# Token layout of a two-layer hybrid backbone: 1154 columns with a gap between the segments, or 1152 columns without one

## The chip, the cores and the metric

The kernel runs on one core of one Trainium2 chip. The metric is the device time of one execution in microseconds (us), as the median of several executions. A core has a matmul engine (PE, with weight loads PEld that overlap the matmuls), three engines for elementwise work (DVE, ACT, POOL), and queues for DMA (SP among them). Each engine works through its own instructions in order and waits on semaphores for the others.

## The reference

Two layers of a diffusion backbone run for two groups of tokens that share all weights: 1024 latent tokens and 128 context tokens, each of 1024 channels. Each layer adds a gated mixer and then a gated feed-forward network (FFN) with a depthwise convolution over three neighbouring tokens. Each group has its own conditioning vector, and a convolution must not reach from one group into the other.

```python
for l in range(DEPTH):                      # 2 layers
    m_ctx = modulation(c_ctx[None, :], w_mod[l], b_mod[l])
    m_lat = modulation(c, w_mod[l], b_mod[l])
    h_ctx = adaln(ctx, g_norm_mix[l], m_ctx[0], m_ctx[1])
    h_lat = adaln(lat, g_norm_mix[l], m_lat[0], m_lat[1])
    # l = 0: latent attention | gMLP;  l = 1: convolution (31 taps) | pooling
    ctx = ctx + m_ctx[2] * mix_ctx
    lat = lat + m_lat[2] * mix_lat
    ctx = ctx + m_ctx[5] * conv_ffn(adaln(ctx, ...), ...)
    lat = lat + m_lat[5] * conv_ffn(adaln(lat, ...), ...)

def conv_ffn(h, w_in, w_dw, b_dw, w_out):   # 1024 -> 2 x 2816 -> 1024
    z = depthwise_conv(h @ w_in, w_dw, b_dw)    # 3 taps, zeros outside the segment
    g, u = z[..., :D_FF], z[..., D_FF:]
    return (jax.nn.silu(g) * u) @ w_out
```

## The kernel before

Activations are held with channels on the partitions and tokens along the row. A row has T = 1154 columns: 1024 latent tokens, two columns of zeros, and 128 context tokens from column CX = 1026. The row is worked in three blocks (BLK): columns 0 to 383, 384 to 767, and 768 to 1153. The third block, block 2, is 386 wide: 256 latent tokens, the two zero columns, 128 context tokens. The normed input `hb` is one tile a block, with rows of BW = 386.

All large products take fp32 operands as a sum of two parts (`split`: ACT writes the high part, L83 or L87; DVE the low part, L84 or L88), and `mm3` (L76 to L78) makes three matmuls for each pair of tiles. Weights come by DMA (`raw`), and `unit_split` splits them too (L66 on ACT, L67 on DVE).

The stages follow one another: norm and projections of layer 0 (`even_kv`, `even_q`, `even_gate`), attention, output projection with the residual and the next norm (`out_half`, `out_blocks`, `norm_blk`), FFN of layer 0 (`ffn`), `odd` for layer 1's mixer, and the FFN of layer 1. In an FFN 44 channel tiles of 128 (22 pairs, g and u) are made one after another; the two tiles of a pair are called its halves. For a half, `products` makes 24 matmuls a block into a PSUM tile (`fps`), and ACT copies each block into the row tile `z` (L405). Two z buffers exist. `half` then scales the row on ACT (L412, the middle tap with the bias) and adds the two neighbours on DVE, over the whole row (L414, L416): the two zero columns keep the segments apart and give the zeros at their ends. `pair` applies SiLU to g (L423) and multiplies (L426), `keep` splits the product (L83, L84) into `act`, and `outp` multiplies two or three of these by the output weights (`ops`), with the residual on DVE (L383, two pieces in block 2).

The two zero columns must be zero wherever a row passes through matmuls: DVE clears them in `hb` (L315, four times), POOL in `gmo`, `att`, `pd` and the convolution's output (L851, L525, L1055, L1251). Their products are zero, so `z` has them without a further instruction.

During the first FFN, DVE also computes later modulation vectors (`mod_fill`, L157), spread between other work by `drip`. Their sums are folded through DRAM, and POOL adds the parts when the DMAs have landed (L167, L168). POOL also adds squares for the norms (L270, L272) and takes the power in the reciprocal root (L589). The order of instructions on each engine is laid out by the tile framework's scheduler, which simulates a time line (`schedule_with_timeline_sim=True`) and takes the ready instruction of the earliest program order; `drip` puts its work later by an offset. A write to a buffer waits for the readers of the tile that had it before.

Of the kernel before, what the change touches and what calls it, by code (L numbers as in the profile page):

```python
# [19 lines left out]
P = 128  # L20
D = 1024
KT = 8
LAT = 1024
CTX = 128
CX = 1026
T = 1154
BLK = [(0, 384), (384, 384), (768, 386)]
BW = 386
TOK = [(i * 128) for i in range(8)] + [CX]
DFF = 2816  # L30
NPAIR = DFF // P
# [12 lines left out]
class Net:  # L44
# [250 lines left out]
    def norm_blk(self, x, l, w, b, hb, pool, big=None, inplace=False):  # L295


        nc = self.nc
        c0, n = BLK[b]
        big = big or {"nsum": (pool, "nsum"), "nsq": (pool, "nsq"), "nt": (pool, "nt")}  # L300

        def tmp(kind):
            p, tag = big[kind]
            return p.tile([P, BW], F32, tag=tag, name=self.nm(kind))

        add, rstd = self.sq_sums([0, 128, 256] if b < 2 else [0, 128, CX - 768], tmp, fast=inplace and b in FASTB)

        rbs = []

        def chain():  # L310
            rbs.append(rstd(D, pool))

        segs = [(0, 384, 0, 0)] if b < 2 else [(0, 256, 0, 0), (CX - 768, 128, 256, 1)]
        if b == 2:
            nc.vector.memset(hb[:, :, :, 256:258].bitcast(F32), 0.0)  # L315

        def scale(out, k, o, m, ro, c):
            nc.vector.scalar_tensor_tensor(out=out, in0=x[:, k, c0 + o:c0 + o + m], scalar=self.scl[l][w][:, k, c:c + 1],
                                           in1=rbs[0][:, ro:ro + m], op0=ALU.mult, op1=ALU.mult)

        def shift(src, k, o, m, c):
            so = 0 if w == 0 else 24
            self.split(hb[:, 0, k, o:o + m], hb[:, 1, k, o:o + m], src, self.mod[l][:, so + k, c:c + 1])

        def rest():
            for k in range(KT):
                for (o, m, ro, c) in segs:
                    t = tmp("nt")[:, :m]
                    scale(t, k, o, m, ro, c)
                    shift(t, k, o, m, c)  # L330

        def scaled():
            for k in range(KT):
                for (o, m, ro, c) in segs:
                    scale(x[:, k, c0 + o:c0 + o + m], k, o, m, ro, c)

        def shifted():
            for k in range(KT):
                for (o, m, ro, c) in segs:
# [47 lines left out]
    def ffn(self, x, l, hb, first, norm=None, after=None, ahead=None):  # L387
        nc, tc, ap = self.nc, self.tc, self.ap
        with ExitStack() as es:
# [4 lines left out]

            def products(tis):

                wz = [(first.pop(0) if first else self.unit(ap["fin"][l, ti]), zp.tile([P, T], F32, tag="z", name=self.nm("z")))
                      for ti in tis]
                for b, (c0, n) in enumerate(BLK):
                    for (wt, z) in wz:  # L400
                        ps = self.gp.tile([P, 512], F32, tag="gp", name=self.nm("fps"))
                        for k in range(KT):
                            self.mm3(ps[:, :n], wt[:, 0, k * P:(k + 1) * P], wt[:, 1, k * P:(k + 1) * P],
                                     hb[b][:, 0, k, :n], hb[b][:, 1, k, :n], k == 0, k == KT - 1)
                        nc.scalar.activation(z[:, c0:c0 + n], ps[:, :n], AF.Copy)  # L405
                return [z for (_, z) in wz]

            def half(ti, i, z=None):
                z = z or products([ti])[0]
                c = cp.tile([P, T], F32, tag="c", name=self.nm("c"))  # L410
                w = self.fdw
                nc.scalar.activation(c, z, AF.Identity, bias=w[:, l, ti, 3:4], scale=w[:, l, ti, 1:2])  # L412
                self.drip(1 if i > 1 else 2)
                nc.vector.scalar_tensor_tensor(out=c[:, 1:T], in0=z[:, 0:T - 1], scalar=w[:, l, ti, 0:1], in1=c[:, 1:T],  # L414
                                               op0=ALU.mult, op1=ALU.add)
                nc.vector.scalar_tensor_tensor(out=c[:, 0:T - 1], in0=z[:, 1:T], scalar=w[:, l, ti, 2:3], in1=c[:, 0:T - 1],  # L416
                                               op0=ALU.mult, op1=ALU.add)
                return c

            def pair(i):  # L420
                zs = products([i, NPAIR + i]) if i < 2 else [None, None]
                g = half(i, i, zs[0])
                nc.scalar.activation(g, g, AF.Silu)  # L423
                self.drip(4 if i > 1 else 8)
                u = half(NPAIR + i, i, zs[1])
                nc.vector.tensor_tensor(out=u, in0=g, in1=u, op=ALU.mult)  # L426
                return u

            def keep(i, u):
                a = cp.tile([P, 2, T], F32R, tag="act", name=self.nm("act"))  # L430
# [32 lines left out]
    def even(self):  # L463
# [5 lines left out]
        with ExitStack() as e1:  # L469
# [45 lines left out]
            with tc.tile_pool(name="at0", bufs=1, side="right", reuse_waits="tile") as p0:  # L515
# [6 lines left out]
                self.drip(1000)  # L522
                self.mod_scale(0, 1)
                att = left.enter_context(tc.tile_pool(name="att", bufs=1, reuse_waits="tile")).tile([P, 4, T], F32, name="att")
                nc.gpsimd.memset(att[:, :, LAT:CX], 0.0)  # L525
                qk = self.att_split(self.hpool, "h2", raw, nc.vector)
                nc.vector.tensor_copy(att[:, :, CX:T], attc)
        self.close("w")
# [317 lines left out]
    def even_gate(self, hb, gmo, w1, w2):  # L846
# [1 line left out]
        nc, ap = self.nc, self.ap  # L848
        load = lambda n, s: self.load(n, s, w1)
        ggv, bs, wst = load("ggv", [P, 512]), load("bs", [P, 512]), load("wst", [P, 4, P])  # L850
        nc.gpsimd.memset(gmo[:, :, LAT:CX], 0.0)  # L851
        wC = [self.unit(ap["evC"][:, s * 1024:(s + 1) * 1024]) for s in range(4)]

        def spatial(gi, vg):
# [186 lines left out]
    def odd(self, x, l, hb, ready):  # L1041
        nc, tc, ap = self.nc, self.tc, self.ap
        with ExitStack() as es:
# [6 lines left out]
            with ExitStack() as e0:  # L1050
# [4 lines left out]
                nc.gpsimd.memset(pd[:, :, LAT:CX], 0.0)  # L1055
                with ExitStack() as e1:
                    w1 = e1.enter_context(tc.tile_pool(name="ow1", bufs=1, reuse_waits="tile"))

# [23 lines left out]
                    def conv_in(i, then=None):  # L1082
# [14 lines left out]

                        def glu(b, ps):
                            c0 = BLK[b][0]
                            for (s, d, n) in ([(0, PADL + c0, 384)] if b < 2 else [(0, PADL + 768, 256), (258, 2 * PADL + LAT, 128)]):  # L1100
                                nc.vector.tensor_tensor(out=cv[:, d:d + n], in0=ps[:, s:s + n], in1=sg[:, c0 + s:c0 + s + n], op=ALU.mult)

                        if i == 0:
# [14 lines left out]
                    def pool(g):  # L1118
                        xp = w1.tile([P, 1184], F32, tag="sg", name=self.nm("xp"))

                        def evac(b, ps):
                            c0 = BLK[b][0]
                            for (s, d, n) in ([(0, 8 + c0, 384)] if b < 2 else [(0, 8 + 768, 256), (258, 24 + LAT, 128)]):
                                nc.scalar.activation(xp[:, d:d + n], ps[:, s:s + n], AF.Copy)

                        proj(evac)
# [119 lines left out]
    def conv_tail(self, b, co, dw, cat, tp, np_, early):  # L1246
        nc = self.nc
        c0 = BLK[b][0]
        segs = [(c0, 0, 384)] if b < 2 else [(768, 0, 256), (COX, CX - 768, 128)]
        if b == 2:  # L1250
            nc.gpsimd.memset(cat[:, :, :, 256:258].bitcast(F32), 0.0)  # L1251
        add, rstd = self.sq_sums([0, 128, 256], lambda kind: (tp if kind == "nsq" else np_).tile([P, BW], F32, tag=kind, name=self.nm(kind)),
                                 have=None if b else early)
        for i in range(0 if b else 3, 4):
# [216 lines left out]
```

## Time and profile before

| | |
|---|---|
| median of 3 runs | 2791.72 us (2788.92 to 2794.14) |
| the profiled execution | 2793.62 us, its span 2791.4 us |
| granted TensorE clock, mean | 0.983 |
| PE busy | 2704.9 us, 15636 matmuls |
| DVE busy | 1839.2 us, 2864 instructions |
| ACT busy | 998.7 us, 1671 instructions |
| POOL busy | 394.6 us, 497 instructions |

The span runs from the first to the last instruction; the execution's own time is 2.2 us longer. A row of the grouped view reads: line, engine, operation, tile written and tiles read, shape, count, then busy time in us, mean duration in ns, and the idle time of the engine just before, with what ended it. A row of a timeline reads: start and duration in us, engine, line, operation, tiles, shape, count, and in brackets the idle time before it. Consecutive rows of one kind are merged.

### The profile page before, as it was taken

The page shows a single profiled execution, that of the slowest core. Times are in us where ns is not written, and L with a number is a line of the kernel's source. Part 1 is how long each engine was busy: PE and PEld are TensorE (multiplying, and loading weights), DVE is VectorE, ACT ScalarE, POOL GpSimd, SP SyncE. Part 2 cuts the span into 40 slices and gives each one's busy share as a digit, 9 for nine tenths or more (in the row PEclk, how much of TensorE's full clock was granted, in tenths as well). Part 3 has the DMA queues.
Part 4 walks back from the last instruction along what each step waited for, and adds up shares of the span by engine and source line. Part 5 has one row for each costly group of instructions (what it writes and reads, how often), then busy time and mean ns, then how long its engine had stood idle before and what let it go on. Part 6 is the DMA issues. An engine that isn't in the chain of part 4 may idle for free.

```text
span 2791.4 us, 38552 instructions
## 1 busy us (share of the span) xinstructions
PE 2704.9 (97%) x15636; PEld 2632.4 (94%) x15636; DVE 1839.2 (66%) x2864; ACT 998.7 (36%) x1671; POOL 394.6 (14%) x497
## 2 busy tenths in 40 slices
PE   7999999999999999999999999989999999999999
PEld 3897989999999999999999999889999999999999
DVE  5873777787786778855553878987555455554445
ACT  3543278782443222222223331324422222222331
POOL 2354165640200000000000200002000000000000
PEclk9999989999999999999999999999999999999999
DMA  7254210006143444311111011010011111111111
GB/s 277 71 151 110 86 37 24 25 11 226 55 125 117 132 129 130 120 46 46 38 46 38 10 46 39 27 53 28 26 40 44 41 43 41 44 38 39 46 46 68
DMA packets 92848, 192.63 MB, mean 69 GB/s; under 512 B 9472, under 2 KB 43136, under 8 KB 92672
## 3 DMA queue, kind: packets, MB, share of 16 engines
q1 hardware_dynamic: 92672, 190.18, 21.6%
q8 instruction: 123, 2.02, 0.3%
q14 instruction: 53, 0.43, 0.1%
HBM read 170.20 MB, written 19.95 MB: 68 GB/s over the span
## 4 chain that ended last, share of the span: by engine, by line
PE 85%; DVE 8%; ACT 2%; DMA 2%; POOL 1%; issue 1%; SPq 0%; DVEq 0%; ACTq 0%; POOLq 0%
PE fps L76 13%; PE fps L77 13%; PE fps L78 13%; PE ops L76 9%; PE ops L77 9%; PE ops L78 9%; PE av L989 2%; PE ptp L978 2%; PE ips L76 1%; PE ips L77 1%; PE ips L78 1%; PE Sa L1002 1%; DVE macc L157 1%; PE Sa L1004 1%; PE Sa L1003 1%
## 5 line engine op out<-in xcount | busy, mean ns | idle before, releaser
L77 PE MATMUL fps<-h,wt 128*128 128x384 f32 (+1 forms) x2112 | 713.2, 338 | 0.0
L76 PE MATMUL fps<-h,wt 128*128 128x384 f32 (+1 forms) x2112 | 711.2, 339 | 1.8 <-ACT h L87 0.9
L78 PE MATMUL fps<-h,wt 128*128 128x384 f32 (+1 forms) x2112 | 712.5, 338 | 0.0
L383 DVE SCALAR_TENSOR_TENSOR x<-ops,mod,x 128x384 f32<-128x384 f32 (+1 forms) x832 | 395.4, 512 | 233.7 <-PE ops L78 231.7
L67 DVE TENSOR_TENSOR wt<-raw,wt 128x1024 fp32r<-128x1024 f32 (+2 forms) x177 | 216.4, 1233 | 391.8 <-ACT wt L66 391.1
L77 PEld LDWEIGHTS fps<-h,wt 128*128 128x128 f32 x2112 | 398.6, 189 | 0.3
L76 PEld LDWEIGHTS fps<-h,wt 128*128 128x128 f32 x2112 | 396.2, 188 | 2.7 <-ACT h L87 1.2
L78 PEld LDWEIGHTS fps<-h,wt 128*128 128x128 f32 x2112 | 398.1, 189 | 0.1
L78 PE MATMUL ops<-act,wt 128*128 128x384 f32 (+1 forms) x1056 | 358.2, 339 | 0.0
L77 PE MATMUL ops<-act,wt 128*128 128x384 f32 (+1 forms) x1056 | 357.0, 338 | 0.0
L76 PE MATMUL ops<-act,wt 128*128 128x384 f32 (+1 forms) x1056 | 355.4, 339 | 0.0
L405 ACT ACTIVATE z<-fps 128x384 f32<-128x384 f32 (+1 forms) x264 | 128.9, 492 | 604.6 <-PE fps L78 604.2
L66 ACT ACTIVATE wt<-raw 128x1024 fp32r<-128x1024 f32 (+2 forms) x177 | 182.9, 1047 | 439.3 <-PE ops L78 322.6
L157 DVE SCALAR_TENSOR_TENSOR macc<-mraw,sc,macc 128x512 f32<-128x512 f32 x280 | 210.8, 783 | 41.5 <-DMA mraw<-in_wmod_dram 40.8
L76 PEld LDWEIGHTS ops<-act,wt 128*128 128x128 f32 x1056 | 199.6, 189 | 0.0
L78 PEld LDWEIGHTS ops<-act,wt 128*128 128x128 f32 x1056 | 198.6, 188 | 0.1
L77 PEld LDWEIGHTS ops<-act,wt 128*128 128x128 f32 x1056 | 198.7, 188 | 0.0
L1200 DVE SCALAR_TENSOR_TENSOR co<-cv,c_odw,co 128x1168 f32<-128x1168 f32 x92 | 132.8, 1446 | 21.0 <-ACT co L1193 20.2
L76 PE MATMUL ops<-h,wt 128*128 128x384 f32 (+1 forms) x384 | 133.1, 353 | 11.5 <-ACT wt L66 7.2
L414 DVE SCALAR_TENSOR_TENSOR c<-z,fdw,c 128x1153 f32<-128x1153 f32 x88 | 127.7, 1452 | 8.6 <-ACT c L412 7.7
L83 ACT ACTIVATE act<-c 128x1154 fp32r<-128x1154 f32 x44 | 51.5, 1172 | 226.7 <-DVE c L426 182.3
L77 PE MATMUL ops<-h,wt 128*128 128x384 f32 (+1 forms) x384 | 132.2, 344 | 0.4 <-DVE h L84 0.4
(281 smaller groups left out, 4550.7 us busy)
## 6 DMA issues: line engine op xcount, KB each, us to landing
raw<-in_fin_dram SPq DMA_DIRECT2D x88, 512.0 KB, 3.5
mraw<-in_wmod_dram SPq DMA_DIRECT2D x160, 256.0 KB, 2.8
raw<-in_fout_dram SPq DMA_DIRECT2D x44, 512.0 KB, 3.5
mraw<-in_wmod_dram SPq DMA_DIRECT2D x16, 512.0 KB, 9.0
fold<-macc SPq DMA_DIRECT2D x14, 512.0 KB, 3.0
macc<-fold SPq DMA_DIRECT2D x56, 128.0 KB, 3.1
x<-in_xt_dram SPq DMA_DIRECT2D x4, 1536.0 KB, 8.9
raw<-in_odin_dram SPq DMA_DIRECT2D x12, 512.0 KB, 3.5
```

The source lines that it names most:

```text
L66: nc.scalar.activation(wt[:, 0, :n], raw[:, :n], AF.Copy)
L67: nc.vector.tensor_tensor(out=wt[:, 1, :n], in0=raw[:, :n], in1=wt[:, 0, :n].bitcast(F32), op=ALU.subtract)
L76: mm(out, wh, ah, start=start, stop=False)
L77: mm(out, wh, al, start=False, stop=False)
L78: mm(out, wl, ah, start=False, stop=stop)
L157: nc.vector.scalar_tensor_tensor(out=a[:, c, :], in0=raw, scalar=self.sc[:, k, c:c + 1], in1=a[:, c, :], op0=ALU.mult, op1=ALU.add)
L383: nc.vector.scalar_tensor_tensor(out=xs, in0=ps[:, o:o + w], scalar=self.mod[l][:, gch * 8 + m, c:c + 1], in1=xs, op0=ALU.mult, op1=ALU.add)
L405: nc.scalar.activation(z[:, c0:c0 + n], ps[:, :n], AF.Copy)
L414: nc.vector.scalar_tensor_tensor(out=c[:, 1:T], in0=z[:, 0:T - 1], scalar=w[:, l, ti, 0:1], in1=c[:, 1:T], op0=ALU.mult, op1=ALU.add)
L978: nc.tensor.transpose(tp[:, a * P:(a + 1) * P], probs[j][:, kt * P:(kt + 1) * P], self.ident)
L989: nc.tensor.matmul(av[:, :256].rearrange("p (j t) -> p j t", j=2), V[:, kt, h, :], rhs, start=(kt == 0 and part == 0), stop=(kt == 8 and p ...
L1200: nc.vector.scalar_tensor_tensor(out=o, in0=cv[:, j:j + COW], scalar=dw[:, j:j + 1], in1=o, op0=ALU.mult, op1=ALU.add)
```

## The change

The row becomes T = 1152 columns, with the context tokens from column 1024, and all three blocks are 384 wide. Only the FFN's z and c tiles keep the gap: they have ZT = 1154 columns and the context part at ZX = 1026. POOL clears the two columns of each z (88 times), the evacuation of block 2 is made in two pieces (256 and 128 columns), and the product of g and u is made in two pieces that close the gap again. The fills of `hb`, `gmo`, `att`, `pd` and the convolution's output go.

```diff
-CX = 1026
-T = 1154
-BLK = [(0, 384), (384, 384), (768, 386)]
-BW = 386
+CX = 1024
+T = 1152
+BLK = [(0, 384), (384, 384), (768, 384)]
+BW = 384
+ZX = CX + 2
+ZT = T + 2
...
-        if b == 2:
-            nc.vector.memset(hb[:, :, :, 256:258].bitcast(F32), 0.0)
...
-                wz = [(first.pop(0) if first else self.unit(ap["fin"][l, ti]), zp.tile([P, T], F32, tag="z", name=self.nm("z")))
+                wz = [(first.pop(0) if first else self.unit(ap["fin"][l, ti]), zp.tile([P, ZT], F32, tag="z", name=self.nm("z")))
                       for ti in tis]
+                for (_, z) in wz:
+                    nc.gpsimd.memset(z[:, LAT:ZX], 0.0)
...
-                        nc.scalar.activation(z[:, c0:c0 + n], ps[:, :n], AF.Copy)
+                        for (o, d, m) in [(0, c0, n)] if b < 2 else [(0, c0, 256), (256, ZX, CTX)]:
+                            nc.scalar.activation(z[:, d:d + m], ps[:, o:o + m], AF.Copy)
...
-                c = cp.tile([P, T], F32, tag="c", name=self.nm("c"))
+                c = cp.tile([P, ZT], F32, tag="c", name=self.nm("c"))
...
-                nc.vector.scalar_tensor_tensor(out=c[:, 1:T], in0=z[:, 0:T - 1], scalar=w[:, l, ti, 0:1], in1=c[:, 1:T],
+                nc.vector.scalar_tensor_tensor(out=c[:, 1:ZT], in0=z[:, 0:ZT - 1], scalar=w[:, l, ti, 0:1], in1=c[:, 1:ZT],
...
-                nc.vector.tensor_tensor(out=u, in0=g, in1=u, op=ALU.mult)
-                return u
+
+                for (d, o, m) in ((0, 0, LAT), (CX, ZX, CTX)):
+                    nc.vector.tensor_tensor(out=u[:, d:d + m], in0=g[:, o:o + m], in1=u[:, o:o + m], op=ALU.mult)
+                return u[:, :T]
...
-                nc.gpsimd.memset(att[:, :, LAT:CX], 0.0)
...
-        nc.gpsimd.memset(gmo[:, :, LAT:CX], 0.0)
...
-                nc.gpsimd.memset(pd[:, :, LAT:CX], 0.0)
...
-        if b == 2:
-            nc.gpsimd.memset(cat[:, :, :, 256:258].bitcast(F32), 0.0)
```

In `odd`, the offsets of the context part within block 2 go from 258 to 256.

More of the change, by code (lines that the diff above doesn't have):

```diff
@@ L413, in half @@
                 self.drip(1 if i > 1 else 2)
-                nc.vector.scalar_tensor_tensor(out=c[:, 1:T], in0=z[:, 0:T - 1], scalar=w[:, l, ti, 0:1], in1=c[:, 1:T],
+                nc.vector.scalar_tensor_tensor(out=c[:, 1:ZT], in0=z[:, 0:ZT - 1], scalar=w[:, l, ti, 0:1], in1=c[:, 1:ZT],
                                                op0=ALU.mult, op1=ALU.add)
-                nc.vector.scalar_tensor_tensor(out=c[:, 0:T - 1], in0=z[:, 1:T], scalar=w[:, l, ti, 2:3], in1=c[:, 0:T - 1],
+                nc.vector.scalar_tensor_tensor(out=c[:, 0:ZT - 1], in0=z[:, 1:ZT], scalar=w[:, l, ti, 2:3], in1=c[:, 0:ZT - 1],
                                                op0=ALU.mult, op1=ALU.add)
@@ L1099, in glu @@
                             c0 = BLK[b][0]
-                            for (s, d, n) in ([(0, PADL + c0, 384)] if b < 2 else [(0, PADL + 768, 256), (258, 2 * PADL + LAT, 128)]):
+                            for (s, d, n) in ([(0, PADL + c0, 384)] if b < 2 else [(0, PADL + 768, 256), (256, 2 * PADL + LAT, 128)]):
                                 nc.vector.tensor_tensor(out=cv[:, d:d + n], in0=ps[:, s:s + n], in1=sg[:, c0 + s:c0 + s + n], op=ALU.mult)
@@ L1122, in evac @@
                             c0 = BLK[b][0]
-                            for (s, d, n) in ([(0, 8 + c0, 384)] if b < 2 else [(0, 8 + 768, 256), (258, 24 + LAT, 128)]):
+                            for (s, d, n) in ([(0, 8 + c0, 384)] if b < 2 else [(0, 8 + 768, 256), (256, 24 + LAT, 128)]):
                                 nc.scalar.activation(xp[:, d:d + n], ps[:, s:s + n], AF.Copy)
```

## The prediction

> **What bounds the kernel now.** First the page: its span, the busy time of each engine, and the chain of work that ended last.
>
> ```profile
> span 2791.4 us, 38552 instructions
> ...
> PE 2704.9 (97%) x15636; PEld 2632.4 (94%) x15636; DVE 1839.2 (66%) x2864; ACT 998.7 (36%) x1671; POOL 394.6 (14%) x497
> ...
> PE 85%; DVE 8%; ACT 2%; DMA 2%; POOL 1%; issue 1%; SPq 0%; DVEq 0%; ACTq 0%; POOLq 0%
> ```
>
> The reader is to see that the matmul engine is busy nearly the whole span and that 85% of the last chain runs through it. Next the table of stretches, with each engine's busy time and instruction count, for the two feed-forward layers and for the norm between layer 0 and layer 1.
>
> ```profile
> core 0: us, PE busy (x) PEld busy (x) DVE busy (x) ACT busy (x) POOL busy (x), PEclk, DMA share, GB/s
> ...
> 800.00:1560.00 760.00, 760.00 (x4331) 759.85 (x4330) 498.59 (x693) 215.10 (x262) 33.79 (x22) 1.00 0.27 84
> 1560.00:1625.00 65.00, 57.63 (x307) 52.87 (x306) 58.51 (x119) 33.89 (x65) 18.02 (x23) 0.99 0.04 14
> ...
> 1960.00:2791.00 831.00, 825.49 (x4684) 824.59 (x4682) 427.76 (x576) 234.35 (x294) 0.00 (x0) 1.00 0.13 43
> ```
>
> In the FFN stretches PE never rests (760.00 of 760.00, 825.49 of 831.00) while DVE, ACT and POOL have much free time. There the time is the number of matmuls times their step, and nothing else. In the stretch 1560:1625 it is different: PE has 7.4 us without work and DVE is busy for 58.5 of 65 us.
>
> **The change, part by part.** *The matmuls of block 2 lose two columns.* The grouped view that keeps shapes apart counts them, one of three equal lines (L76, L77, L78) for each tile:
>
> ```profile
> L78 PE MATMUL fps<-h,wt 128*128 128x386 f32 x704 | 239.1, 340 | 0.0
> ...
> L78 PE MATMUL ops<-act,wt 128*128 128x386 f32 x352 | 119.8, 340 | 0.0
> ...
> L77 PE MATMUL ops<-h,wt 128*128 128x386 f32 x128 | 44.1, 345 | 0.4 <-DVE h L84 0.4
> ...
> L77 PE MATMUL ips<-h,wt 128*128 128x386 f32 x96 | 33.0, 344 | 0.5 <-DVE h L88 0.5
> ...
> L76 PE MATMUL ups<-h,wt 128*128 128x386 f32 x32 | 11.0, 345 | 0.3 <-ACT ug L898 0.3
> ...
> L77 PE MATMUL qps<-h,wt 128*128 128x386 f32 x24 | 8.2, 342 | 0.0
> ```
>
> That is 3 x (704 + 352 + 128 + 96 + 32 + 24) = 4008 matmuls. The mean of 340 ns is of no use here, since matmuls overlap; the step from one to the next is wanted. In the FFN an evacuation (L405) starts as soon as 24 matmuls of its block are done, so its starts in ACT's timeline are a clock for the step:
>
> ```profile
> 1519.78 0.49 ACT L405 ACTIVATE z<-fps 128x386 f32<-128x386 f32 x1 [3.75 <-PE fps L78]
> ...
> 1524.01 0.49 ACT L405 ACTIVATE z<-fps 128x384 f32<-128x384 f32 x1 [1.55 <-PE fps L78]
> ...
> 1528.22 0.49 ACT L405 ACTIVATE z<-fps 128x384 f32<-128x384 f32 x1 [1.59 <-PE fps L78]
> ...
> 1532.47 0.49 ACT L405 ACTIVATE z<-fps 128x386 f32<-128x386 f32 x1 [3.76 <-PE fps L78]
> ```
>
> Block 1 (384) took 4.21 us, block 2 (386) 4.25, block 0 after a block 2 took 4.23; a half of an FFN pair is 12.69 us. The second block is dearer by 0.04 us, so 0.04 / 24 = 1.7 ns a matmul, and 4008 x 1.7 = 6.7 us. This is my value. The upper end charges block 0's 0.02 us to the two columns as well: 0.06 / 24 = 2.5 ns, 10.0 us. The lower end comes from other widths, in PE's timeline:
>
> ```profile
> 231.15 0.40 PE L872 MATMUL vps<-wt,h 128*128 128x512 f32 x1
> ...
> 234.17 0.40 PE L873 MATMUL vps<-wt,h 128*128 128x512 f32 x1
> ...
> 346.10 0.29 PE L1003 MATMUL Sa<-qk 96*128 96x288 f32 x1
> ...
> 346.62 0.29 PE L1004 MATMUL Sa<-qk 96*128 96x288 f32 x1
> ```
>
> The first two rows lie 13 steps of 512 columns apart (232 ns each), the last two 4 steps of 288 (130 ns). The slope is (232 - 130) / 224 = 0.46 ns a column, 0.9 ns for two, 3.6 us in all. I stay with 1.7 ns because its rows are the very matmuls that shrink.
>
> The Trainium skill, page "TensorE: Matmul & The Clock Gate", section "Back-to-back issue gap", gives an isolated warm gap of N/2.4 + 2.5 ns. By it two columns are worth 0.83 ns and the sum would be an estimated 3.3 us, near the lower end above.
>
> *Copies and products that are split in two.* L405 of block 2 becomes 256 and 128 columns (88 times), L426 becomes 1024 and 128 (44 times). The grouped view prices them:
>
> ```profile
> L405 ACT ACTIVATE z<-fps 128x386 f32<-128x386 f32 x88 | 43.3, 495 | 296.2 <-PE fps L78 296.2
> ...
> L980 ACT ACTIVATE PT<-ptp 128x512 fp32r<-128x512 f32 x128 | 73.8, 596 | 19.4 <-PE ptp L978 17.5 <-ACT P L953 0.3
> ...
> L980 ACT ACTIVATE PT<-ptp 128x256 fp32r<-128x256 f32 x32 | 12.4, 388 | 0.0
> ...
> L426 DVE TENSOR_TENSOR c<-c,c 128x1154 f32<-128x1154 f32 x44 | 59.7, 1356 | 0.9
> ...
> L67 DVE TENSOR_TENSOR wt<-raw,wt 128x1024 fp32r<-128x1024 f32 x173 | 212.9, 1241 | 388.2 <-ACT wt L66 387.5 <-PE tp L701 0.6
> ...
> L273 DVE TENSOR_TENSOR nsum<-nsum,nsq 128x384 f32<-128x384 f32 x23 | 13.5, 588 | 22.8 <-POOL nsq L272 22.8
> ```
>
> L980 is the same kind of PSUM copy: 596 - 388 = 208 ns for 256 columns, so 128 columns take about 284. A split evacuation costs 388 + 284 - 495 = 177 ns more, 15.6 us of ACT in 88. For DVE, (1241 - 588) / 640 = 1.02 ns a column puts 128 columns near 327; 1241 + 327 - 1356 = 212 ns more, 9.3 us in 44. Both lie beside matmuls: ACT is busy 215 of 760 us, DVE 499. Without that cover the two would cost 25 us. One place has none, the start of an FFN, where the second pair of z waits for the first:
>
> ```profile
> 780.67 0.88 ACT L405 ACTIVATE z<-fps 128x386 f32<-128x386 f32 x2 [5.22 <-PE fps L78]
> ...
> 788.37 1.28 ACT L423 ACT_TABLE_LOAD   x1 [1.14 <-DVE c L416]
> ...
> 790.74 1.23 ACT L405 ACTIVATE z<-fps 128x384 f32<-128x384 f32 x3
> ...
> L76 PE MATMUL fps<-h,wt 128*128 128x384 f32 x1408 | 476.7, 339 | 0.9 <-ACT z L405 0.9
> ```
>
> Two L405 of block 2 stand ahead of L412, L416 and the next L405, for which PE sat idle 0.9 us. There 2 x 0.177 = 0.35 us come through; with as much in layer 1's FFN (bound: nothing), +0.7 us.
>
> *88 zero fills of z on POOL, and the fills that go.* A POOL fill of about this size takes 0.11 us, one of the removed DVE fills 0.09:
>
> ```profile
> 1523.95 1.42 DVE L416 SCALAR_TENSOR_TENSOR c<-z,fdw,c 128x1153 f32<-128x1153 f32 x1
> 1532.51 0.09 DVE L315 MEMSET h<- 128x32 f32 x1 [7.14 <-PE fps L78]
> 1533.52 0.62 DVE L383 SCALAR_TENSOR_TENSOR x<-ops,mod,x 128x384 f32<-128x384 f32 x1 [0.93 <-PE ops L78]
> ...
> 1618.91 0.10 POOL L1055 MEMSET pd<- 128x8 f32 x1 [14.09 <-DVE h L88]
> 1618.96 0.11 POOL L1094 MEMSET cv<- 128x15 f32 x1
> ```
>
> 88 x 0.11 = 9.7 us of POOL, which is busy 33.8 us in the first FFN and not at all in the second. The fill adds a wait. It cannot start before the last reader of that z buffer, and L412 on ACT waits for it, with L405 and the weight copies L66 queued behind. The reader L416 of the z evacuated at 1519.78 ends at 1525.4; the buffer's next z is complete two halves later, at 1519.78 + 2 x 12.69 = 1545.2. So the fill has 19.8 us. Queued behind it on POOL are the folds' adds (L167, L168), and in the norms L272 and the pow of the rstd. I take nothing. Of the removed fills, the one at 1532.51 held DVE for 7.14 us, but the next instruction waits for PE's first out tile anyway. The DMAs keep their number and queue, and those of block 2 move 0.5% less; I count nothing.
>
> **Sum.** -6.7 + 0.7 = -6.0 us. The profiled execution took 2793.6 us, 2.2 more than its span, and would come to 2787.6. It lies 1.9 above the median of the runs shown, so the median goes from 2791.7 to **2785.7 us**. With the two ends of the column price and 0 to 0.7 for the chain, the forecast's own range is 2781.7 to 2788.8. A measurement of this kernel can tell about 0.2%, 5.6 us, from no change, so the bound lies at 2786.1, almost on the forecast.
>
> **Rivals.** *The step is not set by columns.* A weight load takes longer than the step:
>
> ```profile
> L78 PEld LDWEIGHTS fps<-h,wt 128*128 128x128 f32 x2112 | 398.1, 189 | 0.1
> ```
>
> 189 ns against 4.21 / 24 = 175 ns. If loads set the pace, two columns fewer give nothing, and 0.7 us of chain is left: 2792.4. Against it, the step follows the width (130, 175, 232 ns for 288, 384, 512). The Trainium skill says, in the same section, that in a stream of weight loads and matmuls the spacing is set by both; the steps above do not show the load as the limit at 288 columns and more.
>
> *Norms start earlier.* With the fills L315, L1055 and their like gone, DVE and POOL are free sooner. The stretch 1560:1625 has 7.4 us of idle PE; half of it would make 2785.7 - 3.7 = 2782.0, all of it 2778.3. For it speaks that DVE is the bound there; against it that the instruction behind L315 waited for PE and that the fills behind L1055 were ended by the same norm.
>
> *Slower: the fill comes late.* POOL works in order, and a fold's add can hold what stands behind it:
>
> ```profile
> 696.58 0.53 ACT L257 ACTIVATE nsq<-x 128x384 f32<-128x384 f32 x1 [0.62 <-DVE x L383]
> ...
> 699.20 1.28 POOL L167 TENSOR_TENSOR macc<-macc 128x512 f32<-128x512 f32 x1 [3.80 <-DMA macc<-fold]
> ...
> 701.26 1.01 POOL L272 TENSOR_TENSOR nsq<-nsq,nsq 128x384 f32<-128x384 f32 x1
> ```
>
> The add L272 had its input at 697.1 and ran at 701.3, 4.2 us late, behind L167. A z fill held so would stop L412, behind it L405, and then PE. It decides from a hold of 19.8 us in steady work, and from zero at an FFN's start, where z is short. For slower than 2797.3 some 11.6 us must be lost; three holds of 4.2 us uncovered make 2785.7 + 12.6 = 2798.3. Against it: the cover is over four times the hold that the trace shows.
>
> **How the numbers follow.** Forecast 0.62 (of it 0.55 faster by over 0.2%, since the bound cuts it nearly in half), step not by columns 0.12, earlier norms 0.13, late fill 0.13. Faster: 0.62 x 0.55 + 0.13 = 0.47. Slower: 0.13. Within 0.2%: 0.28 + 0.12 = 0.40. The order on each engine is laid out anew by the kernel's scheduler from its own durations, which moves small waits both ways; the range, from the earlier norms to the first rival, has some 2 us on its upper side for that: 2778 to 2794.
>
> **What would show it.** Right: all fps, act and ups rows at 384 columns, evacuations of block 2 4.21 us after block 1's, a half of 12.63 us, L405 rows of 256 and 128 columns near 388 and 284 ns, 88 POOL fills of z with hardly any ACT idle put down to them. Wrong: a half still at 12.69; PE idle in 800:1560 that ends on z or on a POOL fill; the stretch 1560:1625 grown or shrunk by several us.

## The result, and the profile after

| | before | after |
|---|---|---|
| median | 2792.8 us (2788.9 to 2794.9, 6 runs) | 2774.6 us (2771.9 to 2776.2, 6 runs) |
| ratio | 1 | 0.9935, 95% interval 0.9922 to 0.9947 |
| the profiled execution | 2793.6 us | 2771.9 us |

The change saves 18 us. The forecast was 6 us, and the time lies below its range. The page of the kernel after, with the rows that answer to the first ones of before:

```profile
span 2770.1 us, 39051 instructions
...
PE 2678.3 (97%) x15636; PEld 2605.9 (94%) x15636; DVE 1842.8 (67%) x2904; ACT 1000.8 (36%) x1759; POOL 398.9 (14%) x581
...
PE 77%; DVE 6%; ACT 2%; DMA 2%; issue 1%; POOL 0%; DVEq 0%; SPq 0%; ACTq 0%; POOLq 0%
```

The span is 21.3 us shorter, and PE is busy 26.6 us less for the same 15636 matmuls; so PE rests 5.3 us longer (91.8 instead of 86.5 us). The table of stretches has this row for the first feed-forward layer (columns as before):

```profile
800.00:1560.00 760.00, 760.00 (x4398) 760.00 (x4397) 508.05 (x726) 219.02 (x308) 36.79 (x64) 1.00 0.27 84
```

In the same 760 us, PE never resting, 4398 matmuls start instead of 4331. Two columns fewer in a third of them, at 1.7 ns, would have given some 4331 x 0.57 / 175 = 14 more, not 67. The grouped view with shapes apart shows the added pieces:

```profile
L407 ACT ACTIVATE z<-fps 128x256 f32<-128x256 f32 x88 | 33.9, 385 | 281.6 <-PE fps L80 281.6
L407 ACT ACTIVATE z<-fps 128x128 f32<-128x128 f32 x88 | 24.1, 274 | 0.0
...
L430 DVE TENSOR_TENSOR c<-c,c 128x1024 f32<-128x1024 f32 x44 | 53.7, 1220 | 0.9
...
L430 DVE TENSOR_TENSOR c<-c,c 128x128 f32<-128x128 f32 x44 | 13.6, 309 | 0.0
...
L399 POOL MEMSET z<- 128x2 f32 x88 | 8.7, 100 | 1228.8 <-DVE c L418 1195.3
```

They cost what was forecast (385 and 274 ns for 388 and 284; 309 for 327; a fill 0.10 us for 0.11), and no instruction in the profile waited for a fill. The gain is in the matmuls. The timeline of PE has a row for each, and its start gives the step. Before, the first and the last of 170 matmuls of layer 1's FFN, which take in all three blocks:

```profile
2299.81 0.34 PE L77 MATMUL fps<-h,wt 128*128 128x384 f32 x1
...
2329.60 0.34 PE L78 MATMUL fps<-h,wt 128*128 128x386 f32 x1
```

After, the first and the last of 76 of the same kind, and of the 108 output matmuls behind them in the window:

```profile
2299.81 0.33 PE L80 MATMUL fps<-h,wt 128*128 128x384 f32 x1
...
2312.81 0.33 PE L80 MATMUL fps<-h,wt 128*128 128x384 f32 x1
2312.98 0.34 PE L78 MATMUL ops<-act,wt 128*128 128x384 f32 x1
...
2331.88 0.34 PE L80 MATMUL ops<-act,wt 128*128 128x384 f32 x1
```

Before: 29.79 / 169 = 176.3 ns. After: 13.00 / 75 = 173.3 ns on `hb`, and 18.90 / 107 = 176.6 ns on `act`. The single steps differ too: before, they waver between 168 and 184 ns in this window; after, those on `hb` are all 173 or 174 ns, while those on `act` go back and forth between 174 and 179 or 180. Below, a step is the mean time from one matmul's start to the next one's over all matmuls of a kind in such a timeline, without the few steps over 250 ns, which are waits. By kind of product, with every step that is a wait counted as one of 175 ns, the differences between the two traces add up as follows, to about 20.9 of the 21.3 us:

| product | matmuls | step before | step after | us |
|---|---|---|---|---|
| `fps<-h` (FFN in) | 6336 | 176.2 | 173.4 | -17.6 |
| `ops<-h` (mixers out) | 1152 | 176.6 | 173.6 | -3.3 |
| `ops<-act` (FFN out) | 3167 | 176.1 | 175.2 | -3.1 |
| `ips<-h` (odd mixer in) | 864 | 176.3 | 173.8 | -2.0 |
| all others | | | | -1.3 |
| waits of PE | | | | +6.5 |

In the FFN, block 2 went from 176.9 to 173.4 ns. But blocks 0 and 1, whose matmuls were 384 wide before and after, went from 175.8 to 173.4 ns. That is what the forecast did not have, and the experiments look for its cause. The largest of the changed waits are taken up in the section on the prediction.

### The profile page after: what moved, and what is told of

Its sections match the earlier page's. It is cut to its first block, busy times and chain, and to the rows that moved or that the text cites. A ratio compares the mean times of both kernels' runs of the same rounds, so it can differ in the third digit from the quotient of the medians.

```text
span 2770.1 us, 39051 instructions
## 1 busy us (share of the span) xinstructions
PE 2678.3 (97%) x15636; PEld 2605.9 (94%) x15636; DVE 1842.8 (67%) x2904; ACT 1000.8 (36%) x1759; POOL 398.9 (14%) x581
## 4 chain that ended last, share of the span: by engine, by line
PE 77%; DVE 6%; ACT 2%; DMA 2%; issue 1%; POOL 0%; DVEq 0%; SPq 0%; ACTq 0%; POOLq 0%
PE fps L78 13%; PE fps L79 13%; PE fps L80 13%; PE ops L78 8%; PE ops L79 8%; PE ops L80 8%; PE av L991 2%; PE ptp L980 2%; PE ips L79 1%; PE ips L78 1%; PE ips L80 1%; DMA mraw<-in_wmod_dram 1%; PE Sa L1004 1%; PE Sa L1006 1%; PE Sa L1005 1%; ACT P L955 1%
## 5 line engine op out<-in xcount | busy, mean ns | idle before, releaser
L78 PE MATMUL fps<-h,wt 128*128 128x384 f32 x2112 | 702.6, 335 | 3.3 <-ACT z L407 3.0
L80 PE MATMUL fps<-h,wt 128*128 128x384 f32 x2112 | 705.4, 334 | 0.0
L79 PE MATMUL fps<-h,wt 128*128 128x384 f32 x2112 | 705.1, 334 | 0.0
L80 PE MATMUL ops<-act,wt 128*128 128x384 f32 x1056 | 357.1, 338 | 0.0
L79 PE MATMUL ops<-act,wt 128*128 128x384 f32 x1056 | 356.9, 338 | 0.0
L78 PE MATMUL ops<-act,wt 128*128 128x384 f32 x1056 | 356.2, 339 | 0.0
L159 DVE SCALAR_TENSOR_TENSOR macc<-mraw,sc,macc 128x512 f32<-128x512 f32 x280 | 211.7, 786 | 53.6 <-DMA mraw<-in_wmod_dram 53.1
L399 POOL MEMSET z<- 128x2 f32 x88 | 8.7, 100 | 1228.8 <-DVE c L418 1195.3
L85 ACT ACTIVATE act<-c 128x1152 fp32r<-128x1152 f32 x44 | 51.5, 1171 | 240.7 <-DVE c L430 196.6
L78 PE MATMUL ops<-h,wt 128*128 128x384 f32 x384 | 131.2, 348 | 6.2 <-ACT h L85 4.3
L416 DVE SCALAR_TENSOR_TENSOR c<-z,fdw,c 128x1153 f32<-128x1153 f32 x88 | 124.6, 1417 | 8.7 <-ACT c L414 7.8
```

The costliest lines, as they stand in the source:

```text
L78: mm(out, wh, ah, start=start, stop=False)
L79: mm(out, wh, al, start=False, stop=False)
L80: mm(out, wl, ah, start=False, stop=stop)
L159: nc.vector.scalar_tensor_tensor(out=a[:, c, :], in0=raw, scalar=self.sc[:, k, c:c + 1], in1=a[:, c, :], op0=ALU.mult, op1=ALU.add)
L416: nc.vector.scalar_tensor_tensor(out=c[:, 1:ZT], in0=z[:, 0:ZT - 1], scalar=w[:, l, ti, 0:1], in1=c[:, 1:ZT], op0=ALU.mult, op1=ALU.add)
```

## The experiments

The change that the diff doesn't show as one is in `hb`. It is a tile of 2 x 8 rows a block (two parts, eight channel groups), and each row is the moving operand of a matmul. With BW = 386 rows lie 1544 bytes apart, with 384 they lie 1536 bytes apart. Addresses below are those of the compiled program, in bytes within a partition.

### Row distance alone, and width alone

**e1_pitch386**: the kernel after, with the rows of `hb` 386 columns apart again. All matmuls stay 384 wide, and the order of instructions on PE, DVE, ACT and POOL is the same.

```diff
-        return [self.hpool.tile([P, 2, KT, BW], F32R, tag=f"h{b}", name=self.nm(f"h{b}")) for b in range(3)]
+        return [self.hpool.tile([P, 2, KT, 386], F32R, tag=f"h{b}", name=self.nm(f"h{b}")) for b in range(3)]
```

> The changed kernel with one thing undone: the rows of hb are 386 columns apart again (1544 bytes), while every block keeps 384 columns. Theory COLUMNS (two columns fewer in block 2 made the gain, the addresses do not matter): no change against the changed kernel, 2774.6 us, FFN step 173.4 ns. Theory ADDRESS (rows 1536 bytes apart put every moving operand of hb at the same place within 128 bytes, and the step depends on that place): the step of fps goes back to a mean of 175.8 ns in all three blocks, 8856 matmuls x 2.4 ns = 21 us at most, so 2789 to 2796 us; what then is left below the kernel before is the price of the columns alone.

Measured: 2791.8 us (10 runs), ratio to before 0.9998, interval 0.9989 to 1.0008. The whole gain is gone. In its timeline of PE, the first and the last of 138 matmuls of layer 1's FFN:

```profile
2299.76 0.33 PE L78 MATMUL fps<-h,wt 128*128 128x384 f32 x1
...
2323.73 0.34 PE L80 MATMUL fps<-h,wt 128*128 128x384 f32 x1
```

23.97 / 137 = 175.0 ns. This profiled execution took 2785.6 us, the fastest of its ten, so the others must have had longer steps or waits. What follows: the gain comes with the distance of the rows; without it the two columns, with the copies and fills that they need, leave nothing in the medians. Two reservations. The longer `hb` also moves `act`, whose step in layer 0 went from 173.6 to 176.6 ns (1584 x 3.0 = 4.8 us of the loss). And e1 doesn't price the two columns by themselves: its one trace has 175.1 ns on `hb` in the FFN, against 175.8 and 176.9 before, but its rows also walk through other places than those of before (from 0 to 120 and 128 to 248 bytes above the weights' place modulo 256, where before had 64 to 184 and 192 to 312).

**e7_width386**: the kernel after, with the FFN's matmuls of block 2 made over 386 columns (the last two belong to the next row and aren't used; one in 24 stays at 384).

```diff
-                            self.mm3(ps[:, :n], wt[:, 0, k * P:(k + 1) * P], wt[:, 1, k * P:(k + 1) * P],
-                                     hb[b][:, 0, k, :n], hb[b][:, 1, k, :n], k == 0, k == KT - 1)
+                            w = 386 if b == 2 else n
+                            wl = w if k < KT - 1 else n
...
+                            mm(ps[:, :w], wh_, flat[:, k * BW:k * BW + w], start=k == 0, stop=False)
+                            mm(ps[:, :wl], wh_, flat[:, (KT + k) * BW:(KT + k) * BW + wl], start=False, stop=False)
+                            mm(ps[:, :w], wl_, flat[:, k * BW:k * BW + w], start=False, stop=k == KT - 1)
```

> The changed kernel with the width alone undone in the FFN: the 2112 fps matmuls of block 2 stream 386 columns again, the last two into PSUM columns that nothing reads (they are the head of the next row; one of 24 stays at 384). Pitch and places are those of the changed kernel. Width counts by itself: 2112 x 1.7 = 3.6 us more (at 0.83 to 0.9 ns: 1.9 us), 2776 to 2778 us, blocks 0 and 1 stay at 173.4 ns. Theory EQUAL STREAMS (the fast step needs equal widths as well as one pitch): blocks 0 and 1 go back to some 176 ns too, 6336 x 2.5 = 16 us more, 2790 us.

Measured: 2783.9 us, ratio 0.9965 (0.9951 to 0.9979), 9.3 us more than after. In ACT's timeline the evacuations of blocks 0, 1, 2 and 0:

```profile
1488.54 0.49 ACT L413 ACTIVATE z<-fps 128x384 f32<-128x384 f32 x1 [1.42 <-PE fps L411]
1492.70 0.49 ACT L413 ACTIVATE z<-fps 128x384 f32<-128x384 f32 x1
1496.95 0.55 ACT L413 ACTIVATE z<-fps 128x256 f32<-128x256 f32 x2 [3.77 <-PE fps L411]
1501.12 0.49 ACT L413 ACTIVATE z<-fps 128x384 f32<-128x384 f32 x1 [1.42 <-PE fps L411]
```

Block 2 takes 4.25 us, the others 4.16 and 4.17. Over the trace 386 columns step at 177.0 ns and 384 at 173.65 (173.4 in the kernel after), so two columns cost 3.4 to 3.6 ns, 2112 x 3.6 = 7.6 us, where the rows lie well. There the width counts too, at twice the forecast's price. The 9.3 us are not this price alone. With this edit the scheduler also laid out the instructions in another order. In the trace, the slowest of the five executions, the steps on `act` in layer 1 went from 176.7 to 173.4 ns, 5 us less, though nothing there had moved, and PE's waits grew by 12 us.

**e2_before_pitch384**: the kernel before, with the rows of blocks 0 and 1 1536 bytes apart, and block 2 as it was. A pad puts the rows at the weights' place modulo 128.

```diff
-        return [self.hpool.tile([P, 2, KT, BW], F32R, tag=f"h{b}", name=self.nm(f"h{b}")) for b in range(3)]
+        return [self.hpool.tile([P, 2, KT, (384, 384, 386)[b]], F32R, tag=f"h{b}", name=self.nm(f"h{b}")) for b in range(3)]
...
+            self.hpool.tile([P, 16], F32, name="pad")
```

> The kernel before with one thing of the change: the rows of hb of blocks 0 and 1 are 384 columns apart, with a pad of 64 bytes ahead so that they start at 96 modulo 128 as in the changed kernel; block 2 keeps its 386 columns and its row pitch. COLUMNS: no change, 2792.8 us. ADDRESS: blocks 0 and 1 step at 173.4 ns, block 2 stays near 177; 5904 matmuls x 2.4 ns = 14 us less, 2778.6 us.

Measured: 2792.6 us, ratio 1.0004 (0.9995 to 1.0013); blocks 0 and 1 step at 175.9 ns, as before. Rows at a constant place bring nothing here. Two readings were left: block 2, whose rows walk, holds the other blocks back, or the place that the pad chose is a bad one. The last run (e13) decides.

### The place of the rows

After the change a row's place modulo 256 is the same for all rows of a tile, since 1536 = 6 x 256. Before, 1544 = 6 x 256 + 8 let the place walk by 8 bytes a row. The first seven experiments of this part were laid out with places modulo 128; the reading modulo 256 came from their results.

**e3_act64** pads the c tiles of layer 1 so that `act` moves 192 bytes; **e4_weights_moved** puts all weights 32 bytes lower; **e5_act96** puts `act` at byte 96 modulo 128 in both layers, where `hb` and the weights are; **e6_hb0** and **e8_hb32** move `hb`, and `act` with it, up by 32 and 64 bytes. Nothing else changes; the order on PE, DVE, ACT and POOL is that of the kernel after.

```diff
# e3
-                c = cp.tile([P, ZT], F32, tag="c", name=self.nm("c"))
+                c = cp.tile([P, ZT + 16 * l], F32, tag="c", name=self.nm("c"))[:, :ZT]
# e5
-                c = cp.tile([P, ZT], F32, tag="c", name=self.nm("c"))
+                c = cp.tile([P, ZT + (24, 8)[l]], F32, tag="c", name=self.nm("c"))[:, :ZT]
# e4
+            es.enter_context(tc.tile_pool(name="pad", bufs=1, side="right")).tile([P, 8], F32, name="pad")
# e6; e8 has 16 in place of 8
+            self.hpool.tile([P, 8], F32, name="pad")
```

> The changed kernel with act of layer 1's FFN moved by 192 bytes, from 0 to 64 modulo 128 (16 unused columns more in each c tile of that layer). COLUMNS: no change, 2774.6 us. ADDRESS: the act matmuls of layer 1 (1584) go from 176.7 to 173.6 ns a step as those of layer 0, which have 64 in the changed kernel; 4.9 us less, 2769.7 us, faster than both kernels.

> The changed kernel with all weight tiles 32 bytes lower, at 64 instead of 96 modulo 128; the moving operands stay where they are (hb 96, act 64 in layer 0 and 0 in layer 1). COLUMNS: no change, 2774.6 us. ADDRESS, own place of the moving operand alone: no change of steps (fps 173.4, act 173.6 and 176.7 ns), 2774.6 us. ADDRESS, distance between moving operand and weights: the distance of fps goes from 0 to 32, which act of layer 1 had with 176.7 ns, so 8856 x 3.3 = 29 us more, 2804 us, and act of layer 0 goes to distance 0.

> The changed kernel with act of both FFNs at 96 modulo 128, the place of hb and of the weights (24 and 8 unused columns more in the c tiles of layer 0 and 1); the order of all instructions is that of the changed kernel. Theory DISTANCE (a stream whose moving operand and weights lie at the same place modulo 128 settles at the fast step): act steps at 173.4 ns in both layers, against 173.6 and 176.7 in the changed kernel; 1584 x 3.2 = 5 us less, 2769.5 us. Theory HISTORY (each stretch settles at a fast or a slow step by how it begins, and the place only shifts the odds): act may be at 173.4 or 176.7 in either layer, 2769 to 2780 us.

> The changed kernel with hb 32 bytes higher, at 0 modulo 128, and act with it (96 in layer 0, 32 in layer 1); weights at 96, order of instructions unchanged. DISTANCE: fps has distance 32 as in the run with moved weights, steps between 173.6 and 176.7 ns, up to 2790 us; act of layer 0 has distance 0 and 173.4 ns. HISTORY: some stretches at 173.4, others at 176.7, and not the same layer as there. Only the row pitch matters, not the place: fps at 173.4 ns in both layers, 2774.6 us.

> The changed kernel with hb 64 bytes higher, at 32 modulo 128 (distance 64 from the weights), and act with it (0 and 64); order of instructions unchanged. DISTANCE: fps leaves 173.4 ns, by how much is open; with 176.7 it is 21 us more, 2795 us. Only the row pitch matters: fps at 173.4 ns, 2774.6 us. HISTORY: mixed, 2775 to 2795 us, and the spread of the runs grows.

Measured:

| run | median us | ratio to before, 95% | step on `hb` in the FFN, layers 0 / 1 | step on `act` |
|---|---|---|---|---|
| after | 2774.6 | 0.9935 (0.9922 to 0.9947) | 173.4 / 173.4 | 173.6 / 176.7 |
| e3 | 2774.5 | 0.9940 (0.9925 to 0.9955) | 173.5 / 173.4 | 173.6 / 176.7 |
| e4 | 2783.9 | 0.9977 (0.9967 to 0.9987) | 173.65 / 176.2 | 173.5 / 174.7 |
| e5 | 2765.5 | 0.9905 (0.9890 to 0.9920) | 173.3 / 173.3 | 173.4 / 173.3 |
| e6 | 2780.4 | 0.9957 (0.9943 to 0.9972) | 173.7 / 176.0 | 173.5 / 174.6 |
| e8 | 2766.6 | 0.9911 (0.9896 to 0.9926) | 173.3 / 173.3 | 175.6 / 173.4 |

e5 beats both kernels. In its timeline of PE, the first and the last of 133 output matmuls, where after had 176.6 ns:

```profile
2309.06 0.33 PE L78 MATMUL ops<-act,wt 128*128 128x384 f32 x1
...
2331.94 0.33 PE L78 MATMUL ops<-act,wt 128*128 128x384 f32 x1
```

22.88 / 132 = 173.3 ns. e4 moved the weights down by 32 bytes and e6 moved `hb` up by 32, and both gave nearly the same four steps: it is the distance between the two operands that counts, not the place of either. e3 put layer 1's `act` at the same place modulo 128 as layer 0's, and it stayed slow: a theory with 128 bytes has no answer to that. At distance 32 the FFN's steps on `hb` stayed fast in layer 0 and were slow in layer 1 alone, in e4 and e6 alike: e4's expected 29 us, which counted both layers, became 9, and the theory of history, by which e6 should have had another layer slow, is not borne out.

**e9_off8** and **e10_pitch400** go from e5. e9 moves all rows of `hb` by 8 bytes; e10 spreads the first-part rows of block 0 to 1600 bytes (a small class holds the two parts, so that the rest of the kernel can index them as before).

```diff
# e9
-        return [self.hpool.tile([P, 2, KT, BW], F32R, tag=f"h{b}", name=self.nm(f"h{b}")) for b in range(3)]
+        n = 2 * KT * BW
+        return [self.hpool.tile([P, n + 32], F32R, tag=f"h{b}", name=self.nm(f"h{b}"))[:, 2:2 + n].rearrange("p (a k n) -> p a k n", a=2, k=KT)
+                for b in range(3)]
# e10, in place of the same line
+        out = []
+        for b in range(3):
+            n = KT * (400 if b == 0 else BW)
+            t = self.hpool.tile([P, n + KT * BW], F32R, tag=f"h{b}", name=self.nm(f"h{b}"))
+            out.append(Halves(t[:, :n].rearrange("p (k n) -> p k n", k=KT)[:, :, :BW], t[:, n:].rearrange("p (k n) -> p k n", k=KT)))
+        return out
```

> The kernel with act at byte 96 (2765.5 us, all steps 173.3 ns), with the rows of hb in all three blocks moved by 8 bytes: they stay 1536 bytes apart without gaps, every row now at byte 104 modulo 128 where the weights are at 96. The order of instructions on each engine is the same. Theory place (a moving row must lie on the weights' grid of 64 bytes): the matmuls on hb lose their fast pattern, 175.1 to 177 ns, the 8856 of them cost 16 to 32 us, time 2781 to 2797 us; act matmuls stay at 173.3. Theory walk (the rows' places must not change from row to row, wherever they lie) and theory gaps (rows must follow each other without a gap): 173.3 ns, 2765.5 us.

> The kernel with act at byte 96, with the first-term rows (part 0) of hb block 0 alone 1600 bytes apart instead of 1536: a gap of 64 bytes, places 96 and 32 modulo 128 in turn. The order of instructions on each engine is the same. Theory place: 0 and 64 bytes from the weights are both fast, so all steps stay 173.3 ns and the time 2765.5 us. Theories gaps and walk: block 0 loses the fast pattern, 2952 matmuls at 175.8 to 177 ns cost 7 to 11 us, time 2773 to 2776 us; blocks 1 and 2 stay at 173.3 to 173.7.

Measured: e9 2788.7 us, ratio 0.9988 (0.9978 to 0.9997); e10 2771.4 us, ratio 0.9926 (0.9910 to 0.9943). In e9 nothing walks and no gap lies between rows, and yet most of the gain is gone; so theories "walk" and "gaps" fall. But its blocks differ. The evacuations of blocks 2, 0, 1 and 2 in its timeline of ACT:

```profile
1495.69 0.55 ACT L407 ACTIVATE z<-fps 128x256 f32<-128x256 f32 x2 [3.68 <-PE fps L80]
1499.85 0.49 ACT L407 ACTIVATE z<-fps 128x384 f32<-128x384 f32 x1 [1.42 <-PE fps L80]
1504.12 0.49 ACT L407 ACTIVATE z<-fps 128x384 f32<-128x384 f32 x1 [1.51 <-PE fps L80]
1508.29 0.55 ACT L407 ACTIVATE z<-fps 128x256 f32<-128x256 f32 x2 [3.68 <-PE fps L80]
```

Block 0 takes 4.16 us, block 1 4.27, block 2 4.17. All three lie at byte 104 modulo 128. Modulo 256, blocks 0 and 2 lie at 232 and block 1 at 104, with the weights at 224: distances 8, 136 and 8. (Blocks 0 and 2, both fast, lie an odd multiple of 256 bytes apart, so the period isn't 512.) e10's time lies between what its theories gave. Its block 0 steps at 174.5 ns and the others at 173.8 and 173.4; modulo 256 its rows stand at distances 0, 64, 128 and 192 in turn, not 0 and 64.

### The decision: 128 bytes, a walk between two good places, and the kernel before

**e11_dist128** is e5 with `hb` and `act` moved by 128 bytes; modulo 128 nothing moves. **e12_hi0_lo64** is e5 with 64 bytes between the two parts of each block. **e13_before_dist64** is e2 without its pad: the rows of blocks 0 and 1 then lie at distance 64 modulo 256, where the pad had put them at 128.

```diff
# e11
-            self.hpool = es.enter_context(tc.tile_pool(name="hb", bufs=1, reuse_waits="tile"))
+            self.hpool = es.enter_context(tc.tile_pool(name="hb", bufs=1, reuse_waits="tile")); self.hpool.tile([P, 32], F32, name="pad")
# e12, in place of the line of new_hb
+        out = []
+        for b in range(3):
+            n = KT * BW
+            t = self.hpool.tile([P, 2 * n + 64], F32R, tag=f"h{b}", name=self.nm(f"h{b}"))
+            out.append(Halves(*[t[:, o:o + n].rearrange("p (k n) -> p k n", k=KT) for o in (0, n + 16)]))
+        return out
```

> The kernel with act at byte 96 (all steps 173.3 ns, 2765.5 us), with hb and what lies behind it moved by 128 bytes: rows of hb and act stay 1536 bytes apart and at byte 96 modulo 128, as the weights, but now 128 bytes from them modulo 256, where they were at 0. The order of instructions on each engine is the same. Theory 256 (the step is set by the distance of moving row and weights modulo 256; the act matmuls of the 8-byte run stood at 128 and took 176.0 ns): the 8856 matmuls on hb and the 3168 on act take about 176 ns, 12024 x 2.65 ns = 32 us more, 2797 us (2788 to 2805), no better than the kernel before the change. Theory 128 (only the place modulo 128 counts): 173.3 ns, 2765.5 us.

> The kernel with act at byte 96, with a gap of 64 bytes between the two parts of each hb block: rows of part 0 at distance 0 from the weights modulo 256, rows of part 1 at 64, so that the place of the moving row changes with nearly every matmul (0, 64, 0). act stays at 0. The order of PE's instructions is the same. Theory 256 (0 and 64 were both fast as constant distances): 173.3 to 173.7 ns, 2765.5 us. Theory walk (a change of place from row to row costs): 175 to 177 ns for the 8856 matmuls on hb, 15 to 32 us, 2781 to 2797 us.

> The kernel before, with one edit: the rows of hb blocks 0 and 1 lie 1536 bytes apart instead of 1544, which puts them 64 bytes from the weights modulo 256 (in the earlier run of this kind a pad had put them at 128). Block 2 stays 386 wide with rows 1544 bytes apart. The order of PE's instructions is that of before. Theory 256: 64 is a fast distance, so blocks 0 and 1 step at 173.3 to 174 ns although block 2 walks; 5904 matmuls x 2.4 ns = 14 us, time 2778 us (2775 to 2782); block 2 stays near 177 ns. Theory neighbour (a block whose rows walk holds the blocks behind it back): all blocks stay at 175.9 and above, 2792 us, as in the earlier run.

Measured: e11 2795.1 us, ratio 1.0017 (1.0008 to 1.0027); e12 2770.1 us, ratio 0.9925 (0.9911 to 0.9940); e13 2781.5 us, ratio 0.9968 (0.9953 to 0.9982). In e11's timeline of PE, the first and the last of 164 matmuls of layer 1's FFN:

```profile
2299.84 0.34 PE L79 MATMUL fps<-h,wt 128*128 128x384 f32 x1
...
2328.53 0.34 PE L80 MATMUL fps<-h,wt 128*128 128x384 f32 x1
```

28.69 / 163 = 176.0 ns. A shift of 128 bytes, with every instruction in the same order, costs 29.6 us against e5 (32 were expected) and puts the kernel behind the one before the change. That settles the theory of 256 bytes against that of 128. e12 steps at 173.9 ns on `hb`: a change of place from row to row, between two good distances, costs 0.6 ns and not 1.7 to 3.7. In e13 the evacuations of blocks 2, 0, 1 and 2, in ACT's timeline:

```profile
1503.91 0.49 ACT L405 ACTIVATE z<-fps 128x386 f32<-128x386 f32 x1 [3.76 <-PE fps L78]
1508.07 0.49 ACT L405 ACTIVATE z<-fps 128x384 f32<-128x384 f32 x1 [1.47 <-PE fps L78]
1512.22 0.49 ACT L405 ACTIVATE z<-fps 128x384 f32<-128x384 f32 x1
1516.48 0.50 ACT L405 ACTIVATE z<-fps 128x386 f32<-128x386 f32 x1 [3.76 <-PE fps L78]
```

Blocks 0 and 1 take 4.16 and 4.15 us, block 2 with its walking rows 4.26. So a walking block doesn't hold the others back, and e2 was slow by its place: at distance 128 it had the 175.9 to 176.0 ns of e11. One line in the kernel before, without the change's other parts, thus brings 173.3 ns to two thirds of the matmuls on `hb`. The trace gives 13.4 us of shorter steps (14 were expected) and 6.8 us of longer waits, in the slowest of the five executions, 2786.6 us; by the medians 8.3 us are gained. Those waits weren't followed further.

All constant distances that the runs had, as (moving row - weights) modulo 256, with the steps of 384 columns:

| distance | step in ns, and where |
|---|---|
| 0 | 173.4 after (`hb`); 173.3 e5 (`hb`, `act`), e10 (`act`); 173.4 e12 (`act`); 173.5 e4, e6 (`act` of layer 0) |
| 8 | 173.7 e9 (blocks 0 and 2) |
| 32 | 173.65 and 176.2 e4 (`hb`, layers 0 and 1); 173.7 and 176.0 e6 (the same); 175.6 e8, 176.6 e1 (`act`) |
| 64 | 173.3 e8 (`hb`); 173.3 e13 (`hb`, blocks 0 and 1) |
| 96 | 176.7 e3, 176.6 e1 (`act`) |
| 128 | 176.0 e11 (`hb`, `act`); 176.0 e9 (`act`); 175.9 e2 (`hb`, blocks 0 and 1) |
| 136 | 177.6 e9 (block 1) |
| 160 | 176.7 after, 173.4 e7 (`act` of layer 1) |
| 192 | 174.7 e4, 174.6 e6 (`act` of layer 1) |
| 224 | 173.6 after, e3; 173.7 e7; 173.4 e8 (`act`) |

From 224 over 0 to 64 the matmuls run at 173.3 to 173.7 ns, except at 32; from 96 to 192 at 174.6 to 177.6, except once at 160. Open is why 32 and 160 take one value or the other. At 160, e7 has its instructions in another order than after; at 32, the two values stand in the two layers or in different products. No run tried what decides there, nor what in the chip has the period of 256 bytes.

## Why the prediction was wrong

The step that failed is the first of "the change part by part": "The matmuls of block 2 lose two columns", 4008 x 1.7 = 6.7 us, taken as all that BW = 384 does to PE. It left the step of the other matmuls where it was. The runs show a term that it lacks: the rows of `hb` move from 1544 to 1536 bytes apart, which brings all of them to distance 0 from the weights, and all products on `hb` from 175.8 and 176.9 to 173.4 ns. Undoing the row distance (e1) takes all 18 us back, 4.8 of them by way of `act`; rows 1536 bytes apart in two blocks of the kernel before, with nothing else of the change, bring 8 us at distance 64 (e13) and nothing at distance 128 (e2). So a good place of the rows is part of the gain, and that the change came to one was luck of the layout. The prediction's own rows carried a sign: between 130 ns for 288 columns and 232 for 512, its slope of 0.455 ns puts 384 columns at 130 + 96 x 0.455 = 173.7 ns, and block 1's 4.21 us made 175.4. The prediction asked what a column costs, and not why block 1 stood 1.7 ns above its own slope.

Point by point:

- **PE bounds, and the FFNs set the time**: right. 17.6 of the 27.3 us of shorter steps are `fps`.
- **1.7 ns for two columns**: not a price that carries over. With rows at distance 0 the two columns are worth 3.4 to 3.6 ns (e7). With the rows 1544 bytes apart, e1 as a whole (the narrower block with its copies, `act`'s new place, the rows' other places) gains nothing by its median, and no run prices the two columns there alone. The 4.21 and 4.25 us were a mean over wavering steps. The Trainium skill, page "TensorE: Matmul & The Clock Gate", section "Back-to-back issue gap", gives N/2.4 + 2.5 ns as the isolated warm gap, by which 384 columns would take an estimated 162.5 ns and two of them 0.83 ns. The traces have 173.3 ns at best in this stream of loads and matmuls, and 3.4 to 3.6 for the two, so here the measurements decide.
- **Half of a pair 12.63 us, block 2 4.21 us after block 1**: wrong; 72 x 173.3 ns = 12.48 us, and a block 4.16. The evacuations in the timeline of ACT, blocks 2, 0, 1 and 2:

```profile
1500.09 0.56 ACT L407 ACTIVATE z<-fps 128x256 f32<-128x256 f32 x2 [3.67 <-PE fps L80]
1504.25 0.49 ACT L407 ACTIVATE z<-fps 128x384 f32<-128x384 f32 x1 [1.42 <-PE fps L80]
1508.41 0.49 ACT L407 ACTIVATE z<-fps 128x384 f32<-128x384 f32 x1
1512.57 0.55 ACT L407 ACTIVATE z<-fps 128x256 f32<-128x256 f32 x2 [3.67 <-PE fps L80]
```

- **+0.7 us at an FFN's start**: mis-sized, and from another cause. The waits of PE, between 230 and 797 us, before and then after:

```profile
PE ops L76 <- ACT wt L66: 6.1, 1, 6.1
...
PE fps L76 <- ACT z L405: 0.9, 1, 0.9
...
PE mps L184 <- POOL macc L168: 0.2, 1, 0.2
```

```profile
PE st L283 <- DVE nsum L275: 6.3, 1, 6.3
...
PE fps L78 <- ACT z L407: 3.0, 1, 3.0
PE mps L186 <- POOL macc L170: 1.3, 1, 1.3
```

The wait for z grew from 0.9 to 3.0 us, not by 0.35. The 88 splits are not to blame: in DVE's timeline at that place, before and after, the modulation's sums (L157 before, L159 after) stand otherwise around the first tap (L414, then L416).

```profile
782.82 1.42 DVE L414 SCALAR_TENSOR_TENSOR c<-z,fdw,c 128x1153 f32<-128x1153 f32 x1
...
786.88 1.42 DVE L416 SCALAR_TENSOR_TENSOR c<-z,fdw,c 128x1153 f32<-128x1153 f32 x1
```

```profile
784.73 0.75 DVE L159 SCALAR_TENSOR_TENSOR macc<-mraw,sc,macc 128x512 f32<-128x512 f32 x1 [1.30 <-DMA mraw<-in_wmod_dram]
785.40 1.41 DVE L416 SCALAR_TENSOR_TENSOR c<-z,fdw,c 128x1153 f32<-128x1153 f32 x1
...
789.38 1.41 DVE L418 SCALAR_TENSOR_TENSOR c<-z,fdw,c 128x1153 f32<-128x1153 f32 x1
```

  The first tap now starts at 785.40 instead of 782.82, behind a sum that waited 1.30 us for its DMA. SiLU and the next evacuation follow, and PE. PE also waits 1.3 us, instead of 0.2, for a sum that POOL adds from the folds (L170). The two waits of some 6 us stand at different places: before, PE waits for weights within the output projection, from 636.6 to 643.0 us; after, it runs on there and waits for the norm's sums, from 698.4 to 705.0 us. No run tried these orders by themselves.
- **Splits, fills and removed fills at nothing**: right. No instruction waited for one of the 88 fills of z, so the rival of the late fill falls.
- **Rival, earlier norms**: hardly. PE's waits for DVE's `h` in the odd mixer went from 4.2 to 3.1 us.
- **Rival, the step isn't set by columns**: half right in what it doubted. The step isn't set by columns alone, but neither by the loads, whose mean duration is 188 ns after and 189 before.
- **Range**: its lower end, 2778, was built from the column price and norms that start earlier. A range over "what else does BW touch" was needed; the row distance stood in the diff.

## What to carry to other kernels

When a tile's width changes, ask of each matmul operand what becomes of the distance between its rows and of its place against the weights, before pricing columns. In a kernel like this one, try rows a multiple of 256 bytes apart (1536 here), with the moving tiles at the place of the weights modulo 256 (or 64 bytes above): here a few unused columns (e5) gave 9 us more, half as much as the change. Other types and tile shapes weren't run. And look at matmul starts one by one: a steady sequence (173 and 174 ns) and a wavering one (168 to 184) differ by less than 3 ns in the mean, and yet by 18 us in the whole kernel.

## What the runs showed of the hardware

The step of these fp32 matmuls depends on the distance between the moving row and the weights modulo 256 bytes, 173.3 ns at best and 177.6 at worst for 384 columns, with the granted clock at 1.00 in the FFN. Shifting the moving rows by 128 bytes, with the instructions unchanged, took the kernel from 2765.5 to 2795.1 us (e5, e11). And 386 columns took 177.0 ns at distance 0, where 384 took 173.4 to 173.7 (e7), far more than two columns' share of the step, 0.9 ns.
